# Eleven DMA engines in place of sixteen for one of the last stores

## The chip, the cores and the metric

The kernel runs on one core of one Trainium2 chip. The metric is the device time of one execution in microseconds (us). A core has 16 DMA engines; "engine 5" below means one of these, in the order in which the sync queue's transfers use them. PE, DVE, ACT, POOL and SP are TensorE, VectorE, ScalarE, GpSimd and SyncE.

## The reference

```python
batch, n_heads, seq, head_dim = 8, 12, 1024, 64
def reference(attn_weights, v):       # (8,12,1024,1024), (8,12,1024,64), float32
    return np.einsum('bhqs,bhsd->bhqd', attn_weights, v).astype(np.float32)
```

The weights are 403 MB and are read once. The output is 25 MB.

## The kernel before

96 heads are worked off in 24 groups of four. Loads and most stores are issued from POOL. The last groups are stored from the sync queue. At the end the kernel reads:

```python
store(NV - 4, 2, nc.sync, s_end)                 # 2 MB, rows of 8 KB
store(NV - 2, 1, nc.sync, s_end)                 # 1 MB, rows of 8 KB
rows = osb[:, slot(NV - 1)].rearrange("p (u half j) d -> p u half j d", u=2, half=2)
outs = out_q[NV - 1].rearrange("p (u half j d) -> p u half j d", u=2, half=2, j=GH)
nc.sync.wait_ge(s_out, NU)
nc.sync.dma_start(out=outs[:, 0], in_=rows[:, 0]).then_inc(s_end, 16)   # 512 KB, 128 rows of 4 KB
for k in range(2):                               # 256 KB each, pieces of 1 KB
    nc.sync.wait_ge(s_fin[k], 1)
    js = ds(4 * k, 4)
    nc.sync.dma_start(out=outs[:, 1, :, js], in_=rows[:, 1, :, js]).then_inc(s_end, 16)
# ... (waits for the POOL stores)
nc.sync.wait_ge(s_end, 16 * 5)
```

Twice in the run, 15 tiny transfers with k rows of k+1 words (k = 1 to 15) are issued. Nothing reads their result, but in the trace their packet sizes tell the engines apart:

```python
if n in SMALL_AT:
    for k in range(1, 16):
        nc.sync.dma_start(out=small[0:k, SMALL_AT.index(n), k, 0 : k + 1],
                          in_=ident[0:k, 0 : k + 1]).then_inc(s_small, 16)
```

## Time and profile before

| | before |
|---|---|
| time, median of 6 runs | 1054.86 us (1054.48 to 1055.14) |
| span of the profiled execution | 1052.7 us |
| last load has landed | 1031.19 us |
| last arithmetic (a copy on DVE) ends | 1043.25 us |
| last store has landed | 1051.00 us |

The kernel is bound by its bytes: the DMA engines are full from the start to 1048 us. Only the last three microseconds are ragged. The prediction shows the lines for this.

### The profile page before, as it was taken

The page shows a single profiled execution, that of the slowest core. Times are in us where ns is not written, and L with a number is a line of the kernel's source. Part 1 is how long each engine was busy: PE and PEld are TensorE (multiplying, and loading weights), DVE is VectorE, ACT ScalarE, POOL GpSimd, SP SyncE. Part 2 cuts the span into 40 slices and gives each one's busy share as a digit, 9 for nine tenths or more (in the row PEclk, how much of TensorE's full clock was granted, in tenths as well). Part 3 has the DMA queues.
Part 4 walks back from the last instruction along what each step waited for, and adds up shares of the span by engine and source line. Part 5 has one row for each costly group of instructions (what it writes and reads, how often), then busy time and mean ns, then how long its engine had stood idle before and what let it go on. Part 6 is the DMA issues. An engine that isn't in the chain of part 4 may idle for free.

```text
span 1052.7 us, 16310 instructions
## 1 busy us (share of the span) xinstructions
PE 731.2 (69%) x6920; PEld 685.8 (65%) x6920; DVE 388.6 (37%) x582; ACT 397.7 (38%) x485; POOL 45.1 (4%) x80
## 2 busy tenths in 40 slices
PE   0877677676687677657768658776766865975985
PEld 0767676566687567656668557765666865865874
DVE  0543344333353234333335324433333433532542
ACT  0443344433353334423335324433333533533543
POOL 1000000000000000000000000000000000000000
PEclk9989888898798888879879878888887987988998
DMA  9999999999999999999999999999999999999998
GB/s 239 220 217 219 219 242 219 219 219 246 229 219 252 212 217 256 219 219 232 245 214 214 253 217 219 259 219 218 252 215 214 217 213 226 219 207 229 207 216 339
DMA packets 14779, 240.21 MB, mean 228 GB/s; under 512 B 1716, under 2 KB 2228, under 8 KB 5172
## 3 DMA queue, kind: packets, MB, share of 16 engines
q0 software_dynamic: 12912, 233.84, 99.0%
q1 hardware_dynamic: 1860, 6.30, 1.6%
q8 instruction: 2, 0.03, 0.0%
q14 instruction: 5, 0.04, 0.0%
HBM read 427.82 MB, written 25.17 MB: 430 GB/s over the span
## 4 chain that ended last, share of the span: by engine, by line
DMA 78%; PE 20%; issue 1%; POOL 0%; DVE 0%; ACT 0%; POOLq 0%; SPq 0%
DMA abf<-in_attn_weights_dram 78%; PE bank L132 19%; PE bank L174 0%; PE bank L159 0%; POOL abf L319 0%; DVE osb L239 0%; ACT ot L268 0%; POOLq L446 0%; SPq L391 0%; SPq L83 0%
## 5 line engine op out<-in xcount | busy, mean ns | idle before, releaser
L132 PE MATMUL bank<-ident,abf 128*128 128x128 f32 x3072 | 447.2, 316 | 278.4 <-DMA abf<-in_attn_weights_dram 274.5
L132 PEld LDWEIGHTS bank<-ident,abf 128*128 128x128 f32 x3072 | 437.7, 214 | 291.3 <-DMA abf<-in_attn_weights_dram 286.6
L256 DVE COPY at<-bank 128x1024 bf16<-128x1024 bf16 x480 | 320.1, 689 | 469.6 <-PE bank L132 468.4
L256 ACT COPY at<-bank 128x1024 bf16<-128x1024 bf16 x288 | 288.7, 1012 | 428.5 <-PE bank L132 428.5
L174 PE MATMUL bank<-at,vbf 128*64 128x256 bf16 x3072 | 215.0, 278 | 0.0
L174 PEld LDWEIGHTS bank<-at,vbf 128*64 128x64 bf16 x3072 | 196.8, 108 | 13.4 <-DVE at L256 4.0
L268 ACT COPY ot<-bank 128x512 f32<-128x512 f32 x48 | 28.1, 586 | 181.0 <-PE bank L174 181.0
L268 DVE COPY ot<-bank 128x512 f32<-128x512 f32 x48 | 33.2, 692 | 151.4 <-PE bank L174 151.4
L159 PE MATMUL bank<-ident,ot 128*128 128x128 f32 x392 | 52.2, 276 | 32.9 <-DVE vbf L232 32.2
L159 PEld LDWEIGHTS bank<-ident,ot 128*128 128x128 f32 x392 | 43.4, 141 | 45.0 <-DVE vbf L232 44.0
L239 ACT COPY osb<-bank 128x512 f32<-128x512 f32 x97 | 52.2, 589 | 22.5 <-PE bank L159 22.5
L319 POOL DMA_DIRECT2D abf<-in_attn_weights_dram x50 | 27.3, 546 | 686.9 <-PE bank L132 685.9
L232 DVE CAST vbf<-bank 128x512 bf16<-128x512 f32 x48 | 30.9, 686 | 6.6 <-PE bank L147 6.6
L232 ACT CAST vbf<-bank 128x512 bf16<-128x512 f32 x48 | 25.8, 589 | 11.9 <-PE bank L147 11.9
L147 PE MATMUL bank<-vr,spread 32*128 32x512 bf16 x384 | 25.8, 377 | 0.0
L325 POOL DMA_DIRECT2D vr<-in_v_dram x11 | 7.8, 706 | 241.7 <-PE bank L147 241.7
L147 PEld LDWEIGHTS bank<-vr,spread 32*128 32x128 bf16 x384 | 10.1, 92 | 6.8
L309 DVE CAST vr<-osb 128x4096 bf16<-128x4096 f32 x1 | 2.3, 2294 | 22.9 <-DMA osb<-in_v_dram 22.9
L332 POOL DMA_DIRECT2D out_dram<-osb x10 | 7.2, 717 | 28.6 <-ACT osb L239 28.6
L256 ACT ACT_TABLE_LOAD x4 | 5.1, 1283 | 1.1 <-SPq L83 1.1
L356 POOL TENSOR_SCALAR_AFFINE_SELECT spread<-spread 32x512 bf16<-32x512 bf16 x4 | 2.5, 632 | 0.6
L239 DVE COPY osb<-bank 128x512 f32<-128x512 f32 x1 | 0.7, 693 | 3.1 <-PE bank L159 3.1
(8 smaller groups left out, 2.1 us busy)
## 6 DMA issues: line engine op xcount, KB each, us to landing
abf<-in_attn_weights_dram POOLq DMA_DIRECT2D x46, 4096.0 KB, 33.8
out_dram<-osb POOLq DMA_DIRECT2D x10, 2048.0 KB, 29.4
vr<-in_v_dram POOLq DMA_DIRECT2D x11, 1024.0 KB, 17.2
abf<-in_attn_weights_dram POOLq DMA_DIRECT2D x4, 2048.0 KB, 24.1
osb<-in_v_dram SPq DMA_DIRECT2D x1, 2048.0 KB, 24.4
out_dram<-osb SPq DMA_DIRECT2D x1, 2048.0 KB, 13.7
out_dram<-osb SPq DMA_DIRECT2D x1, 1024.0 KB, 15.9
out_dram<-osb SPq DMA_DIRECT2D x1, 512.0 KB, 11.5
```

What stands on the lines that cost most here:

```text
L132: last = pe.matmul(out=pt[g % 4][:, k], lhsT=words[:, k], rhs=ident, is_transpose=True, start=(k == 0), stop=(k == KW - 1),)
L147: last = pe.matmul(out=ps, lhsT=spread[rows, b], rhs=vr[rows, two, b], start=(b == 0), stop=(b == VB - 1),)
L159: last = pe.matmul(out=ps[:, ds(j * P, P)], lhsT=ot[:, j0 + j], rhs=ident, is_transpose=True, start=(j == 0), stop=(j == jn - 1),)
L174: last = pe.matmul(out=outs, lhsT=vbf[:, 2 * kw + par, h], rhs=at[:, ds(half * GH, GH), kw, ds(h * VP, VP), par], start=(n == 0), stop=(n ...
L232: copy(out=vbf[:, :, h], in_=ps.rearrange("p (k d) -> p k d", k=SB)).then_inc(s_vbf[e])
L239: return copy(out=rows.rearrange("p (half j) d -> p j half d", half=2)[:, ds(j0, jn)], in_=ps[:, ds(0, jn * P)].rearrange("p (j half d) -> ...
L256: ins = copy(out=at[:, g].rearrange("c k j two -> c (k j two)"), in_=bank[g % 4].bitcast(bf16),)
L268: copy(out=ot.rearrange("c j (h p) -> c h j p", h=VH)[:, ds(2 * e, 2)], in_=po[e].rearrange("c (h j p) -> c h j p", h=2, j=GH),).then_inc( ...
L319: pool.dma_start(out=abf[n % 2][:, ds(g0, gn)].rearrange("p g s -> p (g s)"), in_=attn_q[n // 2][:, ds((n % 2 * G + g0) * S, gn * S)],).th ...
L325: pool.dma_start(out=vr.rearrange("p two b x -> p two (b x)"), in_=v_2[iv]).then_inc(s_v, 16)
L332: eng.dma_start(out=out_2[q // 2] if fours == 2 else out_q[q], in_=at_slot if fours == 2 else at_slot[:, 0], **({"single_packet": True} if ...
L356: pool.affine_select(out=spread[ds(h * VP, VP)], in_=spread[ds(h * VP, VP)], compare_op=mybir.AluOpType.not_equal, fill=1.0, base=0, patte ...
```

## The change

The intent is to relieve the engines that finish last. The 512 KB store is cut into one of 121 rows and one of 7, so that it runs on the eleven lowest engines, 11 or 12 rows each, and not on engines 11 to 15.

```diff
-        nc.sync.dma_start(out=outs[:, 0], in_=rows[:, 0]).then_inc(s_end, 16)
+        for p0, pn in ((0, 121), (121, 7)):
+            nc.sync.dma_start(
+                out=outs[ds(p0, pn), 0], in_=rows[ds(p0, pn), 0]
+            ).then_inc(s_end, 16)
...
-        nc.sync.wait_ge(s_end, 16 * 5)
+        nc.sync.wait_ge(s_end, 16 * 6)
```

## The prediction

> **What bounds the kernel now.** I read the page first: its slices, its queues and the chain that ended last.
>
> ```profile
> DMA  9999999999999999999999999999999999999998
> ...
> q0 software_dynamic: 12912, 233.84, 99.0%
> q1 hardware_dynamic: 1860, 6.30, 1.6%
> ...
> DMA abf<-in_attn_weights_dram 78%; PE bank L132 19%; PE bank L174 0%; PE bank L159 0%; POOL abf L319 0%; DVE osb L239 0%; ACT ot L268 0%; POOLq L446 0%; SPq L391 0%; SPq L83 0%
> ```
>
> The 16 DMA engines are busy in all forty slices and the chain is made of loads of the weights: the kernel is as long as its bytes take. The change moves no byte of a load. It can act only where the engines are no longer all busy, and the last slice, the only 8, says that there is such a place. So I went to the end: what the sync queue waited for, the timeline of its issues, and the busy time in stretches after the last load.
>
> ```profile
> SPq L419 <- DMA out_dram<-osb: 7.3, 1, 7.3
> SPq L415 <- ACT osb L239: 5.4, 1, 5.4
> SPq L411 <- ACT osb L239: 4.8, 1, 4.8
> ```
>
> ```profile
> 1031.28 0.93 SPq L332 DMA_DIRECT2D out_dram<-osb  x2
> ...
> 1036.98 0.34 SPq L411 DMA_DIRECT2D out_dram<-osb  x1
> ...
> 1042.73 0.97 SPq L415 DMA_DIRECT2D out_dram<-osb  x2
> ```
>
> ```profile
> 1042.70:1048.00 5.30, 0.00 (x0) 0.00 (x0) 0.55 (x1) 0.01 (x1) 0.00 (x0) 0.89 1.00 413
> 1048.00:1049.00 1.00, 0.00 (x0) 0.00 (x0) 0.00 (x0) 0.00 (x0) 0.00 (x0) 0.50 0.93 335
> 1049.00:1050.00 1.00, 0.00 (x0) 0.00 (x0) 0.00 (x0) 0.00 (x0) 0.00 (x0) 0.50 0.24 84
> 1050.00:1051.00 1.00, 0.00 (x0) 0.00 (x0) 0.00 (x0) 0.00 (x0) 0.00 (x0) 0.50 0.09 31
> ```
>
> (The columns before the last two of a stretch are the five engines and the granted clock; the last two are the DMA share and GB/s.) The last arithmetic ends at 1043.25 us, but the wait of L419 for all stores takes 7.3 us more. Until 1048 the engines are full, working off a backlog of stores. Then the share falls to 0.24 and to 0.09, which is one or two engines of sixteen. The wait ends at 1051.0, the span at 1052.7. So the stores' end is ragged: most engines are done two microseconds before the last.
>
> **Which engines are late.** No view prints a DMA engine's number, so I worked from the records behind the views. (1) Each DMA counts its semaphore up once per engine. In every load of the second half of the run, 12 counts come within some 0.5 us, and the two last 2.0 us after the first; from about 750 us on two others come 0.8 us after it. The load that lands at 1019.5 has its four last at 0.86, 1.16, 2.00 and 2.02 us. (2) Packets of one engine follow without a gap, so each engine is a chain. The small transfers of L395 have k rows of k+1 words, k from 1 to 15, so that the smallest packet in a chain names its engine: a chain whose smallest is 52 bytes (k=12) is engine 11. In the second set (915 to 951 us) the two late chains start with 52 and 56 bytes: **engines 11 and 12**. The two middle ones start with 12 and 16 bytes: engine 0 or 1 (these two can't be told apart), and engine 2. (3) From 1028 us on, I split the packets into sixteen chains, each made to hold the five sync stores in order; all packets fit. The last packets end:
> - engines 11 and 12: 1050.66 and 1050.67
> - the two middle ones: 1049.50 and 1049.80
> - one at 1049.44, and eleven from 1048.58 to 1049.08.
> The counts arrive 0.33 us after the packet (1051.00 for 1050.67).
>
> The lag is not the stores' doing. The gap of 1.2 us is there after the two 16 KB packets of the instruction queue (at 44 and 56 us, 0.94 and 0.97 us long), and one engine of the middle pair falls back by 0.3 us when an 8 KB instruction packet (0.32 us) comes at 754 us, and again at 1018.8 us (two such packets, at 601 and 896 us, leave no mark on this pair). An engine that is never idle carries such a delay to the end.
>
> **What the Trainium skill says.**
> - "DMA: Bandwidth & Descriptors", section "Why a DMA increments its semaphore by 16 and not by 1": the number of engines is the largest k up to 16 that divides the slowest dimension, and on the sync queue they are the lowest-numbered k. So 128 rows go on 16 engines, 8 each; 121 rows on engines 0 to 10, 11 each; 7 rows on 0 to 6. This trace agrees as far as it goes: in the small transfers the packets of 64 bytes number 30, two sets of 15 engines, and those of 52 bytes 24, two of 12.
> - The same page, "Queues, rings and completion order": an engine takes turns between its queues, a packet at a time, and each queue is in order. The trace agrees: while loads run, a small packet appears once per load packet, about every 2.42 us.
> - The same page, "Latency and other measured facts", calls engines 7 and 15 usually slower. Here that is not so: 11 and 12 are late, and by delays, not by a slower rate.
> - The same page, "Issuing engines are not separate DMA queues": all queues end on the same 16 engines. So moving a store helps only by moving it between engines.
>
> **The change part by part.** The half's 512 KB (128 rows of 4 KB) are the same. What moves is who carries them. A chain of eight 4 KB packets takes 1.25 us in the trace (1046.42 to 1047.67), so a row is 0.156 us.
> - Engines 11 to 15 lose 8 rows: 8 x 0.156 = 1.25 us earlier. For 11 and 12: 1050.67 - 1.25 = 1049.42.
> - Engines 0 to 6 get 11 + 1 = 12 rows, 4 more: 0.62 us later, and one more count packet (under 0.01 us). Engines 7 to 10 get 3 more: 0.47 us.
> - The middle pair is among 0 to 6, so its later one goes from 1049.80 to **1050.43**. The others of 0 to 10 end at most at 1049.44 + 0.63 = 1050.07.
> - The two 256 KB stores stand behind the half in each ring and are unchanged. No engine runs dry for want of them: they are issued from 1042.73, and an engine that drops the half still has the older stores until about 1046.
> - One more issue on the sync queue (0.34 us by the issue it replaces) lies in the 5.4 us wait ahead of L415, so it costs nothing. The wait counts to 96 in place of 80, with no time of its own. PE, DVE, ACT and POOL run the same instructions in the same order.
>
> The end moves from engines 11 and 12 to one of engines 0 to 2: 1050.67 becomes 1050.43. Gain **0.24 us**, of 2.09 us of raggedness (1050.67 - 1048.58). From the median of 1054.88 that is 1054.6 us.
>
> **The rivals.**
> - The whole gain of the late engines, 1.25 us (near 1053.6 us): if the middle pair's lag is of the profiled run, or of other engines, as it stems from instruction packets. The end would then be near 1049.75, counts included. For it: the lag of 11 and 12 is old and stable, that of the middle pair late and made by single packets. Against: 0.8 us of it stands in each load's counts from 758 us on, as stable as the other from there.
> - The low engines become a worse end than the one removed (1055.2 to 1056): if the two late engines are other ones in an unprofiled run, 0.63 us is added where the end is set, or if 11 neighbouring rows on an engine are fetched slower than 8. For 12 rows at 0.19 instead of 0.156 us the low engines would lose 0.4 us more. Nothing in the profile speaks for a slower row: a 4 KB packet lasts 0.159 us whatever else runs.
> - Hidden anyway (1054.9): the end is set by the fixed 0.33 us and by the last two stores, not by the half. Against: in the late chains packets follow without a gap up to the last, so any row taken off them shows.
> - An engine as the bound: excluded, the PE ends at 1042.5 with nothing behind it but a copy.
>
> **Range and chances.** The sum gives 1054.6. The three runs before spread over 0.66 us, more than the gain, and the rivals reach 1053.6 and 1055.5. I take 1053.9 to 1055.2. Two per cent is 21 us, ten times the whole ragged end, so "within" is all but certain.
>
> **What would show it right or wrong.** In the changed profile: the last two counts of the final store no longer stand 0.7 us alone; engines 11 and 12 end near 1049.4 and one or two low ones near 1050.4; the share in the last microsecond before the end is again one or two engines, while the share a microsecond earlier rises, as eleven engines work longer (from 0.24 to some 0.6); the wait of L419 shrinks from 7.3 to 7.0-7.1 us; everything before 1037 us stands. Wrong if the lags fall on other engines in that run, if 4 KB packets get longer than 0.159 us, or if the loads' own end (1031.2 us) moves by more than the tail gains.

## More of the kernel before

One line of the timeline matters later: the transposes of the last load, with the idle time ahead of them and what ended it.

```profile
1031.27 4.14 PE L132 MATMUL bank<-ident,abf 128*128 128x128 f32 x32 [1.84 <-SPq L391]
```

PE turns the last 32 tiles in 4.14 us once the last load is in, and this sets when the last two stores can be issued.

## The result and the profile after

| | before | after |
|---|---|---|
| time, median of 6 runs | 1054.86 us (1054.48 to 1055.14) | 1055.24 us (1054.36 to 1055.72) |
| span of the profiled execution | 1052.7 us | 1052.6 us |
| last store has landed, profiled execution | 1051.00 us | 1050.85 us |

The ratio is 1.0002, with a 95% interval of 0.9989 to 1.0015: the same. (A ratio is the mean time of one kernel's runs over that of the other's of the same rounds, so it is not quite the ratio of the medians.) The six runs of the changed kernel are not one heap, however: 1054.36 and 1054.45, then 1055.23, 1055.26, 1055.44 and 1055.72. The profile is of the first.

What the sync queue waited for in the changed kernel (total, times, longest):

```profile
SPq L413 <- ACT osb L239: 6.2, 1, 6.2
SPq L419 <- ACT osb L239: 5.0, 1, 5.0
SPq L423 <- DMA out_dram<-osb: 4.0, 1, 4.0
```

Its last stretches, with the columns of the prediction's lines (the last two are DMA share and GB/s):

```profile
1042.70:1048.00 5.30, 1.06 (x8) 0.86 (x8) 0.69 (x1) 0.99 (x2) 0.00 (x0) 0.79 0.98 409
1048.00:1049.00 1.00, 0.00 (x0) 0.00 (x0) 0.00 (x0) 0.00 (x0) 0.00 (x0) 0.50 0.89 323
1049.00:1050.00 1.00, 0.00 (x0) 0.00 (x0) 0.00 (x0) 0.00 (x0) 0.00 (x0) 0.50 0.56 198
1050.00:1051.00 1.00, 0.00 (x0) 0.00 (x0) 0.00 (x0) 0.00 (x0) 0.00 (x0) 0.50 0.04 15
```

And from its timeline, the last load's transposes and the issues:

```profile
1031.61 5.59 PE L132 MATMUL bank<-ident,abf 128*128 128x128 f32 x32 [3.30 <-SPq L391]
...
1031.63 0.93 SPq L332 DMA_DIRECT2D out_dram<-osb  x2
...
1038.78 0.71 SPq L413 DMA_DIRECT2D out_dram<-osb  x2
...
1044.53 2.35 SPq L419 DMA_DIRECT2D out_dram<-osb  x2
```

Three things are to be seen. The share between 1049 and 1050 us rises from 0.24 to 0.56: more engines work longer. The share after 1050 falls from 0.09 to 0.04: 16 x 0.04 is 0.64 us of engine time, one engine to 1050.53 and one to 1050.15. And the last two stores are issued at 1044.53, 1.8 us later than before, because PE took 5.59 us for the transposes in place of 4.14. This goes with PE's idle time before them, 3.30 us in place of 1.84, as PE was done earlier with the load before. In the traces below 1.83 us of idle time goes with 4.14 us, and 3.30 or 3.31 us with 5.40 to 5.59. The Trainium skill, "TensorE: Matmul & The Clock Gate", section "Part 1: The HAM clock gate (the "warmup" mystery)", has the clock halved after an idle window of about 3.4 us. The granted clock from 1031 to 1042.7 us is indeed 0.85, where it was 1.00 before. But 3.30 us is less than that window, and the transposes at 1011.9 us of the kernel before took 5.59 us after an idle time of only 2.06 us. So when the clock falls is not settled by these traces. It is not the change's doing: nothing before 1037 us was touched, and the second trace of the changed kernel has 1.83 us and 4.14 us. The second of the two issues also took 1.80 us in place of 0.42. The end did not wait for either, as the next paragraph shows. The wait of L423 is shorter than before mostly because it starts later.

The packets, split into chains as in the prediction, end so. The last engine has 12 rows: its 1 MB store ends at 1047.30, its 11 rows at 1049.01, its one row at 1049.17, its two last stores at 1049.85 and 1050.53, each step being as long as the packets take, without a gap. Engines 11 and 12 end their 1 MB store at 1048.26 and 1048.42; with 0.68 us for each last store this makes 1049.6 and 1049.8, no longer the end. Before they ended at 1050.66 and 1050.67. In this execution the change did what it was made for. Four of the other five, at 1055.23 to 1055.72 us, show no gain in their time.

### The profile page after: what moved, and what is told of

Same layout as the page of the kernel before. It is cut to its first block, busy times and chain, and to the rows that moved or that the text cites. A ratio compares the mean times of both kernels' runs of the same rounds, so it can differ in the third digit from the quotient of the medians.

```text
span 1052.6 us, 16311 instructions
## 1 busy us (share of the span) xinstructions
PE 736.8 (70%) x6920; PEld 691.4 (66%) x6920; DVE 388.5 (37%) x582; ACT 397.9 (38%) x485; POOL 45.1 (4%) x80
## 4 chain that ended last, share of the span: by engine, by line
DMA 77%; PE 21%; issue 1%; POOL 0%; DVE 0%; ACT 0%; SPq 0%; POOLq 0%
DMA abf<-in_attn_weights_dram 77%; PE bank L132 21%; PE bank L174 0%; PE bank L159 0%; POOL abf L319 0%; DVE osb L239 0%; ACT ot L268 0%; POOLq L450 0%; SPq L83 0%; SPq L391 0%
## 5 line engine op out<-in xcount | busy, mean ns | idle before, releaser
L132 PE MATMUL bank<-ident,abf 128*128 128x128 f32 x3072 | 452.8, 318 | 274.6 <-DMA abf<-in_attn_weights_dram 269.2
L132 PEld LDWEIGHTS bank<-ident,abf 128*128 128x128 f32 x3072 | 443.4, 215 | 287.5 <-DMA abf<-in_attn_weights_dram 281.3
```

What stands on the lines that cost most here:

```text
L132: last = pe.matmul(out=pt[g % 4][:, k], lhsT=words[:, k], rhs=ident, is_transpose=True, start=(k == 0), stop=(k == KW - 1),)
```

## The experiments

There were eleven runs, one of them of the changed kernel once more. Each kernel was timed beside the kernel before on the same chip, and every trace is of the first execution listed. Except where said, only the row split of the half differs. All results were correct.

**The changed kernel again.** No edit.

> The changed kernel once more, unedited. Six runs of it spread from 1054.36 to 1055.72 us. Theory A (only the balance of the engines counts): mean 0.2 to 0.3 us under the kernel before, and the spread is chance. Rival B (the added DMA on the sync queue costs something in some runs): mean 0.2 to 0.6 us over the kernel before, with a part of the runs near 1055.3. In the profile, under either: the two late engines are no longer last, the last count is that of an engine with 12 rows, near 1050.7 to 1050.9 us.

Runs: 1054.33, 1054.59, 1055.85, 1054.24, 1056.07 us; the kernel before 1054.64 to 1055.19 in nine. So there are again two groups. With the six runs above: five of the changed kernel's eleven lie near 1054.4, six near 1055.6 (means 1054.39 and 1055.60). A mean of the groups says nothing of either. In the trace the last count is at 1050.81, with the late pair out of the way, as expected.

**Two halves of 64 rows**, each on all 16 engines.

```diff
-        for p0, pn in ((0, 121), (121, 7)):
+        for p0, pn in ((0, 64), (64, 64)):
```

> The store in two DMAs of 64 rows, each on all 16 engines with 4 rows: the engine loads of the kernel before, with the six DMAs of the changed one. Theory A (balance): like the kernel before within 0.1 us, end of the last packet near 1050.67, late engines alone in the last 0.7 us. Rival B (cost of the sixth DMA): 0.2 to 0.6 us slower than the kernel before, with a long (over 1 us) issue of the last store on the sync queue as in the changed kernel's profile (1.80 us).

Runs: 1054.61, 1055.03, 1055.04, 1054.63, 1054.98, mean 1054.86 against 1054.84 for the kernel before. The second of the last two issues is long here too (2.75 us for the pair, in the line below), and it costs nothing. Theory B falls: neither the sixth DMA nor its long issue is what makes slow runs.

```profile
1044.07 2.75 SPq L419 DMA_DIRECT2D out_dram<-osb  x2
```

This also agrees with the Trainium skill, "DMA: Bandwidth & Descriptors", section "Rules for kernel authors", which says of two transfers to disjoint partition halves that they share the same engines, so that nothing is won: 0.02 us here.

**64, 55 and 9 rows**: 4 rows on all engines, 5 on the eleven lowest, 1 on the nine lowest.

```diff
+        for p0, pn in ((0, 64), (64, 55), (119, 9)):
...
+        nc.sync.wait_ge(s_end, 16 * 7)
```

> 64 rows on 16 engines (4 each), 55 on engines 0 to 10 (5 each), 9 on engines 0 to 8: the late engines 11 and 12 lose 4 rows, engines 0 to 8 get 2 more, 9 and 10 one more. Theory A: late engines end at 1050.67 - 4 x 0.156 = 1050.05, the later middle one at 1049.80 + 0.31 = 1050.11, so 0.55 us faster than the kernel before (1054.3) and 0.3 us faster than the changed one. Rival B: seven DMAs, no faster than the changed kernel, 0.2 us or more slower than the kernel before.

Runs: 1054.25, 1055.84, 1054.20, 1055.64, 1054.43. The three fast ones have a mean of 1054.29, right where theory A put them (1054.3). The two slow ones are 0.8 and 1.0 us over the kernel before. Balancing works, on some executions.

**125 rows on five engines, 3 on three.**

> 125 rows on the five lowest engines (25 each) and 3 rows on three: engines 0 to 2 get 18 rows more than in the kernel before. If a row costs the engine 0.156 us here too and a low engine of the middle pair (1049.80 in the kernel before) is among 0 to 2: last packet at 1049.80 + 2.81 = 1052.6, so 1.9 us slower than the kernel before (1056.8). If no middle engine is among 0 to 2 the end is 1049.08 + 2.81 = 1051.9, 1.2 us slower. If the row is dearer on few engines (0.19 us): 2.5 us slower.

Runs: 1056.81, 1059.30, 1057.97, 1056.93. The two fast ones are where the sum put them (1056.8). The slow ones are 1.1 and 2.4 us above these. The profiled execution's last packet ends at 1052.98 (expected 1052.6).

So an execution can be slow by one or two microseconds when low engines carry more. Three causes remained. In theory C the late engines are 11 and 12 in the profiled execution but others elsewhere. In theory H the rows themselves are slower in some executions. In theory F the last two stores come late.

**127 rows on one engine.**

```diff
+        for p0, pn in ((0, 127), (127, 1)):
```

> 127 rows of the half on engine 0 alone (and one row split over 16 engines, which is next to nothing): the run's time is then engine 0's own backlog plus 127 rows. A row at 0.156 us: 1047.5 + 19.8 = 1067.3 us for the last packet if engine 0 is a normal one (1048.5 + 19.8 = 1068.3 if it is the middle one that engine 0 or 1 is), about 1071.4 (1072.4) us in time. The runs of the changed kernel fall in two groups about 1.2 us apart, those of the kernel before do not. Theory C (in other executions the late engines are low ones): the runs of this kernel lie within 2.0 us of each other, as no lag is longer. Theory H (in some executions the 4 KB rows themselves go slower, about 0.1 us each): some runs are 8 to 12 us longer than others. Theory F (in some executions the last two stores are issued late): no spread beyond 0.5 us, as these stores have 15 us to spare.

Runs: 1071.19, 1071.81, 1071.32, 1071.59, 1071.75: a single group, where theory H needed 8 to 12 us between some. The trace shows the 4 KB packets 0.155 us apart, to the end. (The single row did not split over 16 engines, as I had expected. All 128 packets of 4 KB are there, none of 256 B.) Engine 0 begins its half at 1046.09, so it is not late: the middle one of engines 0 and 1 is engine 1. Up to 1052 and from about 1060 the share is 0.06: engine 0 is alone, one of sixteen. In between the others write their last two stores:

```profile
1048.00:1052.00 4.00, 0.00 (x0) 0.00 (x0) 0.00 (x0) 0.00 (x0) 0.00 (x0) 0.50 0.06 27
1052.00:1056.00 4.00, 0.00 (x0) 0.00 (x0) 0.00 (x0) 0.00 (x0) 0.00 (x0) 0.50 0.25 87
1056.00:1060.00 4.00, 0.00 (x0) 0.00 (x0) 0.00 (x0) 0.00 (x0) 0.00 (x0) 0.50 0.25 88
1060.00:1065.00 5.00, 0.00 (x0) 0.00 (x0) 0.00 (x0) 0.00 (x0) 0.00 (x0) 0.50 0.06 26
```

What delayed these to after 1052 is in the sync queue's issues:

```profile
1038.64 13.53 SPq L413 DMA_DIRECT2D out_dram<-osb  x2
1052.22 3.64 SPq L419 DMA_DIRECT2D out_dram<-osb  x2
```

The second DMA of the half took 13.22 us to issue: the queue stood until engine 0 had only 88 of its rows left. In this trace a deep backlog on one engine thus held up the sync queue for all.

**Five engines, the last two stores on the ACT queue.** They are taken out of the sync queue. The cut shows what is added.

```diff
+            for k in range(2):                      # on ACT, at its end
+                nc.scalar.wait_ge(s_fin[k], 1)
+                nc.scalar.dma_start(out=..., in_=...).then_inc(s_end, 16)
```

> The 25 rows on five engines again, but with the two last 256 KB stores issued on the ACT queue. With all on the sync queue the runs were 1056.81, 1056.93, 1057.97 and 1059.3. Theory F (the last stores are issued late in some executions, held up in the sync queue): all runs within 0.4 us, near 1056.8. Theory C (late engines are low ones in some executions): two groups still, 1056.8 and up to 1057.7. Theory H (slower rows): two groups still, up to 1059.3.

Runs: 1056.81, 1056.92, 1056.72, 1056.70 and 1059.17. Four are in one group, and one is slow by 2.4 us all the same. Theory F falls as the cause: in this kernel nothing of the last two stores can be held up in the sync queue. But the slow run is 1.5 us over what theory C allowed (1057.7), and near the 1059.3 that theory H had.

**The changed kernel, the last two stores on the ACT queue.**

> The changed kernel with the two last 256 KB stores on the ACT queue. Theory F: one group of runs, near 1054.4, and the gain of 0.25 to 0.4 us over the kernel before is there in the mean. Theories C and H: two groups as in the changed kernel, near 1054.4 and 1055.3 to 1056.

Runs: 1054.51, 1057.21, 1055.70, 1055.79, 1055.58. The first execution is fast, the others are not. The mean is 0.6 us over that of the kernel before. Theory F falls once more. The run of 1057.21 lies above the 1055.3 to 1056 of theories C and H too.

**120 rows on fifteen engines, 8 on eight.**

> 120 rows on engines 0 to 14, 8 each as in the kernel before, and 8 rows on engines 0 to 7: uneven in the same two DMAs as the changed kernel, but no engine has more than 9 rows. Theory C (the engines that come late are 11 and 12 in the profiled execution, but others in other executions, and a kernel is only exposed to it where it gives low engines more): all runs within 0.7 us of each other and within 0.3 us of the kernel before, no run over 1055.6. Theory U (an uneven half on the low engines by itself makes some executions slow): some runs 0.8 us or more over the kernel before, as in the changed kernel and the one of 64, 55 and 9 rows.

Runs: 1054.78, 1055.42, 1055.42, 1055.10, 1055.98; the kernel before 1054.93 to 1055.41. The expectation of theory C missed: the runs lie within 1.2 us, not 0.7, and one is over 1055.6. By theory U there should have been a group 0.8 us over the kernel before. There is one such run. The mean is 0.24 us over the kernel before, for one row more on eight engines (0.155 us). It does not decide.

**122 rows on two engines, 6 on six.**

> 122 rows on engines 0 and 1, 61 each, 6 rows on engines 0 to 5: 54 rows more than before on engines 0 and 1. One of them is the middle engine (1049.80): last packet 1049.80 + 54 x 0.156 = 1058.2, time 1062.4. Theory C: runs that are slow are so by at most 0.9 to 2.4 us (a late engine in place of the middle one), however many rows; one run in four or five. Theory H2 (rows go slower where several low engines carry many, about 0.09 us a row): slow runs 4 to 6 us over the fast ones.

Runs: 1062.40, 1062.41, 1062.96, 1062.57, 1062.40: where the sum put them (1062.4). The largest spread is 0.56 us with 54 rows more on each of two engines, where slower rows (theory H2) would have made 4 to 6 us. So rows are not slower on two engines. It does not follow for more engines: with five, 18 rows more made slow runs of 1.1 and 2.4 us.

**Early copies on eleven engines, even half.** This takes the tail out of the question. The kernel before, its half on 16 engines, gets two copies of 55 rows on engines 0 to 10, halfway through the run. They write rows that the last stores overwrite.

```diff
+            if n == 30:
+                for p0 in (0, 55):
+                    nc.sync.dma_start(
+                        out=out_q[NV - 1][ds(p0, 55), 0:1984],
+                        in_=v_q[NV - 1][ds(p0, 55), 0:1984],
+                    ).then_inc(s_early, 16)
...
+        nc.sync.wait_ge(s_early, 32)
         store(NV - 4, 2, nc.sync, s_end)
```

> The kernel before with an even half (8 rows on every engine at the end), but with two copies of 55 rows of 7.9 KB on engines 0 to 10 in the middle of the run, 10 rows and about 3 us of work on each of these engines (their result is overwritten at the end). Theory C: the low engines are now the late ones in the profiled execution, with 3.0 us more of lag; in other executions, where the naturally late engines are among the low ones, the two lags add up: two groups of runs, 0.8 us or more apart, the slow ones in the majority. Theory U (only the uneven half at the end does it): one group, spread at most 0.6 us, near 1054.9 + 2.2 = 1057.1.

Runs: 1056.87, 1056.91, 1057.25 and 1058.38, 1058.62. These are two groups, with no uneven store at the end. Theory U falls: it is enough that the low engines carry more, here halfway through the run. Theory C had the slow runs in the majority, and they are two of five. In the profiled execution (a fast one), of the 16 counts of the load that lands at 1030 us, three come within 0.3 us, two at 1.8 us and eleven 2.6 to 3.6 us after the first: by their number engines 13 to 15, the late pair, and the eleven with the copies. So the delay given halfway stays to the end, as the natural lags do. The last microseconds show many engines ending late together:

```profile
1050.00:1051.00 1.00, 0.00 (x0) 0.00 (x0) 0.00 (x0) 0.00 (x0) 0.00 (x0) 0.70 0.81 319
1051.00:1052.00 1.00, 0.00 (x0) 0.00 (x0) 0.00 (x0) 0.00 (x0) 0.00 (x0) 0.50 0.76 272
1052.00:1053.00 1.00, 0.00 (x0) 0.00 (x0) 0.00 (x0) 0.00 (x0) 0.00 (x0) 0.50 0.31 109
```

**The same copies on all sixteen**, 64 rows each, as a control.

```diff
-                for p0 in (0, 55):
+                for p0 in (0, 64):
```

> Control for the kernel with the early copies on eleven engines, whose runs fell in two groups (1056.87, 1056.91, 1057.25 and 1058.38, 1058.62): the same copies with 64 rows each, on all 16 engines, 8 rows on each. Theory C (two lags add up where the early copies sit on the low engines only): one group, spread at most 0.7 us as in the kernel before, near 1055 + 2.4 = 1057.4. If the added copies by themselves make some executions slow: two groups again, 1.2 us or more apart.

Runs: 1057.75, 1057.46, 1057.26, 1057.15, 1057.13. This is one group, within 0.62 us, where theory C put it (1057.4). Its 8 rows per engine cost 2.44 us (1057.35 - 1054.91 in the means), or 0.305 us a row. The slow group of the eleven-engine kernel is 3.4 us over its kernel before (1058.50 - 1055.10), which is somewhat more than its whole 10 rows (3.05): by theory C the added work lies fully on top of the longest lag there. The fast group is only 1.9 us over it (1057.01): in its trace the longest lag lies on engines that got no copy.

## Why the prediction was right or wrong

**In the profiled execution the sum held.** Its last packet was put at 1050.43 and ended at 1050.53. The late pair was put at 1049.42, and came out at 1049.6 and 1049.8. Its lag in the last load was larger in this execution, 2.16 and 2.28 us in place of 2.00 and 2.02. The row of 0.156 us was measured as 0.155. The share of 0.6 between 1049 and 1050 came as 0.56. The last count fell by 0.15 us (1051.00 to 1050.85), where 0.24 was said, and the time of the traced executions by 0.16 us (1054.52 to 1054.36). The fast group's mean, 1054.39, is 0.2 us under the predicted 1054.6, but this group was picked by its outcome.

**The median was not that of the profiled execution.** The step that failed, as far as is known, is the choice of the executions that the sum stands for. The prediction put the second rival ("if the two late engines are other ones in an unprofiled run, 0.63 us is added where the end is set", 1055.2 to 1056) behind the sum and made 1054.6 its centre. Six of eleven runs of the changed kernel lie at 1055.2 to 1056.1, at a mean of 1055.60, where 1054.86 + 0.63 makes 1055.5. The median of the first six, 1055.24, is 0.04 us above the range of 1053.9 to 1055.2, and their mean, 1055.08, is inside it. That is partly luck: the range was made wide for the rivals, and the gain at its centre is not there in the mean. The interval of the ratio is some 1.4 us to either side, so the timing alone could not have shown a gain of 0.24 us. "Within 2%" was right, and was never in doubt.

**How far the cause is shown.** Shown is that slow groups come only with an uneven load on the low engines: the even kernels, including the one with two halves and the one with sixteen early copies, stay within 0.8 us in any set of runs. The uneven load need not be at the end (the early copies), and neither the sixth DMA, nor its issue, nor the last stores' place in the sync queue makes the slow runs. Slower rows are excluded on one and on two engines. A rival that no run excludes is that rows go slower in some executions when five or more low engines carry more.

What I take for the cause, argued and not shown, is theory C: an execution has one or two engines with a lag of about 2 us, and these are not the same in each execution. The kernel before gives every engine the same, so it does not matter to it which are late. By this theory the changed kernel wins 0.24 us where they are among 11 to 15 and loses up to 0.63 us where they are among 0 to 6. The frequencies point the same way, weakly: no clear slow run in ten with one or two loaded engines (1062.96 is the nearest), three in nine with five, twelve in twenty-one with eleven loaded at the end (the changed kernel, the one with 64, 55 and 9 rows, and the one with the ACT queue).

In size the theory falls short. The kernel before has the longest lag in it whichever engine is late, so an uneven kernel can be over it by no more than its added rows take. This is 0.31 us for 64, 55 and 9 rows, 0.62 us for the changed kernel, and 2.81 us for five engines. Against the means of the kernel before, the slow runs are over it by 0.8 and 1.0 us, by 0.4 to 1.2 us, and by 3.1 to 4.5 us. So the slow runs need longer lags than the traces show, or a second cause.

**What stays open.** No trace shows late engines other than 11 and 12, since all traces are of first executions, and all of the first executions with uneven stores fell into the fast group. So that the late engines change place is argued, not shown. Nor is the first execution a fair sample: in the seven series with two groups 18 of 35 runs are fast, and yet all seven first ones are, which chance would give about once in 170 times (the product of the seven fast shares). What sets it apart, be it the profiler or being first, no run tells. Three runs (1059.30 and 1059.17 with five engines, 1057.21 with the ACT queue) are 1.2 to 1.7 us slower than their added rows can make them. The kernel with fifteen engines spread more than the theory allowed. Why the issue of the last store takes 1 to 2 us in most kernels with more than five DMAs stays open too; no trace shows that it moved an end.

**Smaller steps.** The wait of L423 was to shrink to 7.0 or 7.1 us and was 4.0, since its start moved: the last issue came 1.8 us later with PE's clock and stood 1.8 us. That the other queue's issue is free held. Of the middle engines, the one of 0 or 1 is engine 1. The other was named engine 2. In the changed kernel's trace two chains of about this lag, both at 1046.91 after the 1 MB store, part ways, one with 12 rows and one with none, so which of them it is there I can't say.

**Two readings of the prediction.** "The lag is not the stores' doing" holds for the first 1.2 us of it. The lag of the last two counts of a load behind the first count is 1.25 us at 129 us of the kernel before, then 1.48 at 149, 1.84 at 236 and 2.07 at 323, and about 2.0 us from there on. The three steps come at the loads that follow the stores issued from POOL at 125.0, 213.1 and 299.6 us, and no instruction packet is on record there. And the 30 packets of 64 bytes are no evidence for two sets of 15 engines, as 15 rows make as many packets on any number of engines. The rule itself (the Trainium skill, "DMA: Bandwidth & Descriptors", section "Why a DMA increments its semaphore by 16 and not by 1", on the number of engines and the lowest-numbered ones) agreed where it could be checked: 127 rows went on one engine (128 packets with those of a one-row DMA, 0.155 us apart), and the last engine of the changed kernel had 11 rows and one.

## What to carry to other kernels

Before work is moved between DMA engines to suit a trace, ask whether the late engines are late in every execution: the trace shows one. Time it in enough runs to see groups and not only a median, and amplify the imbalance until the groups stand clear of each other. Where the late engines may be any, the even split is the one that loses nothing; here five of eleven uneven runs lie half a microsecond under the even kernel's median (1054.39 against 1054.86) and six lie three quarters over it (1055.60).

## What the Trainium skill lacked or had wrong

- "Runtime: NRT & Kernel Launch", section "Instruction fetch mechanics", says that a sequencer fetches its instructions by its own DMA queue in blocks of 16 KiB, at a cost that is "mostly hidden". The trace of the kernel before has two such blocks (0.94 and 0.97 us) and five packets of 8 KB (0.32 us each) in the run. It does not agree with the cost where the DMA engines are the bound. There such a block is work for an engine that is never idle: after the two blocks two engines lag by 1.2 us, and the lag is there, grown to 2.0 us, to the end. The 3 us of copies given halfway to eleven engines stayed to the end in the same way.
- "DMA: Bandwidth & Descriptors", section "Latency and other measured facts", names engines 7 and 15 as usually slower. Here the two late ones are 11 and 12 in the ten traces where the tiny packets let me name both, and by a delay, not by a rate: in the kernel before the lag is 2.07 us at 323 us and 2.02 us in the last load.
- No page that I found says that one engine's backlog can stop the issuing queue: with 127 rows on engine 0 the next issue took 13.22 us, until 88 rows were left.
- No page that I found says that a traced first execution may not stand for the later ones. The runs show it only by their groups: 1054.4 and 1055.6 us for one and the same kernel, with every first run in the fast group.
